# One word of the output through a register of SyncE: eight register instructions at the end of a kernel bound by its loads

## The chip, the cores and the metric

One core of a Trainium2 chip. The time is device microseconds (us) of one execution. A profile's span is shorter than the time of the same execution (711.54 against 709.78 in the kernel before). Times that are read from a trace count from the span's start. Those of single closing instructions are given to 0.01 us, as the trace has them; the views print them to 0.1.

## The reference

```python
def setup_inputs():
    B, N = 8, 2176
    return {"a": np.random.randn(B, N, N).astype(np.float32),
            "b": np.random.randn(B, N, N).astype(np.float32)}

def reference(a, b):
    prod = np.matmul(a, b)
    traces = np.diagonal(prod, axis1=1, axis2=2).sum(axis=-1)
    return traces.astype(np.float32)
```

Only the traces of eight products are wanted, so each is the sum of `a` transposed times `b`, element by element. The output is eight float32 words.

## The kernel before

GpSimd issues the loads, which convert to bf16 on the way. PE transposes blocks of `a`; ScalarE and VectorE copy them out of PSUM; VectorE multiplies with `b` and sums. For the last matrix PE takes a part of the products, and the last row of `b` comes in three pieces. What the change touches is the end:

```python
    # ... const pool: ones, sums [128 x 8], late [128 x 4], result [128 x 8] ...
    late_acc = tiles["late"]
    for n, (x, y) in enumerate(late):
        multiply_reduce(x, y, late_acc[:, n:n + 1])
    multiply_reduce(tiles[f32], trace_ps, late_acc[:, len(late):len(late) + 1])

    total = psum_small.tile([1, BATCH], f32, tag="total")
    nc.tensor.matmul(
        total[:, 0:BATCH - 1], tiles["ones"], tiles["sums"][:, 0:BATCH - 1],
        start=True, stop=True,
    )
    parts = [tiles["sums"][:, BATCH - 1:BATCH]] + [late_acc[:, n:n + 1] for n in range(len(late) + 1)]
    for n, part in enumerate(parts):
        nc.tensor.matmul(
            total[:, BATCH - 1:BATCH], tiles["ones"], part,
            start=(n == 0), stop=(n == len(parts) - 1),
        )
    nc.vector.tensor_copy(out=tiles["result"][:1, :BATCH], in_=total)      # 128 partitions summed by PE
    nc.sync.dma_start(
        out=out.rearrange("(a b) -> a b", a=1),
        in_=tiles["result"][:1, :BATCH],
    )
```

## Time and profile before

| | before |
|---|---|
| time, median of 3 runs | 711.72 us (711.46 to 711.79) |
| span of the profiled run | 709.8 us |
| loads issued by GpSimd, share of 16 engines' span | 100.1% |
| last load lands | 705.60 us |
| VectorE's last copy | 706.91 to 707.06 us |
| SyncE issues the output | 707.10 to 707.42 us |
| end of the span | 709.78 us |

The table is read in two parts. Up to 705.60 the loads set the pace, and other engines have room. From there on a short chain of dependent steps runs to the end. After the kernel's own instructions comes closing code that all carries the line of the launch: SyncE checks off the semaphores of all engines and DMAs, and then all engines meet twice. (A semaphore is a counter that one instruction raises and another waits on.) The lines of the page, the chain, the timeline and SyncE's waits are in the prediction.

### The profile page before, as it was taken

To read this page: it belongs to the slowest core of one execution; us is meant where nothing else is said; L and a number is where in the kernel's file an instruction comes from. 1 tells how busy PE (TensorE), PEld (TensorE's weight loads), DVE (VectorE), ACT (ScalarE), POOL (GpSimd) and SP (SyncE) were. 2 spreads that over 40 slices of the span, in tenths; PEclk is the share of its full clock that TensorE was granted. 3 is DMA by queue.
4 is the path that set the end of the run, shared out by engine and by line. 5 is a ranking of instruction groups with operands and counts; after the bars stand their busy time and mean duration, and the time that the engine had idled before them with its cause. 6 is when DMAs were issued, how large, how long until landed. Compare 5 with 4: busy or idle time off the path is not lost.

```text
span 709.8 us, 3800 instructions
## 1 busy us (share of the span) xinstructions
PE 233.3 (33%) x1406; PEld 221.8 (31%) x1406; DVE 408.9 (58%) x449; ACT 201.6 (28%) x210; POOL 45.2 (6%) x91
## 2 busy tenths in 40 slices
PE   2660025600345003540036400374003630036356
PEld 1660025600344003540036400374003630036355
DVE  0327972279812898219972199621996319963146
ACT  2651015600256002550035500354003630036300
POOL 2000000000000000000000000000000000000010
PEclk9866556755588555885556755666556875567755
DMA  9999999999999999999999999999999999999997
GB/s 220 220 220 219 206 219 219 220 218 206 221 219 218 218 210 218 220 218 214 213 219 219 218 213 214 220 218 216 213 217 219 218 216 212 218 218 216 219 210 139
DMA packets 12116, 152.32 MB, mean 215 GB/s; under 512 B 1346, under 2 KB 1602, under 8 KB 3778
## 3 DMA queue, kind: packets, MB, share of 16 engines
q0 software_dynamic: 11952, 150.97, 100.1%
q1 hardware_dynamic: 146, 1.11, 0.4%
q8 instruction: 11, 0.18, 0.1%
q14 instruction: 7, 0.06, 0.0%
HBM read 303.04 MB, written 0.00 MB: 427 GB/s over the span
## 4 chain that ended last, share of the span: by engine, by line
DMA 52%; issue 43%; POOL 3%; PE 2%; DVE 1%; another core or an unknown queue 0%; POOLq 0%; DVEq 0%
DMA t<-in_a_dram 42%; DMA t<-in_b_dram 6%; DMA b_t<-in_b_dram 3%; POOL t L57 2%; PE ps L136 1%; PE trace_ps L256 1%; DVE scratch L103 0%; DVE at L91 0%; POOL b_t L222 0%; POOLq L57 0%; PE ps L157 0%; POOL identity masks.py:199 0%; PE total L271 0%; POOL identity masks.py:197 0%
## 5 line engine op out<-in xcount | busy, mean ns | idle before, releaser
L103 DVE CUSTOM_DVE_ANT_1 scratch<-at,t 128x2048 bf16<-128x2048 bf16 (+1 forms) x156 | 310.5, 1990 | 85.5 <-DMA t<-in_b_dram 78.9
L136 PE MATMUL ps<-identity,t 128*128 128x128 f32 x1071 | 204.2, 372 | 460.3 <-DMA t<-in_a_dram 297.7
L136 PEld LDWEIGHTS ps<-identity,t 128*128 128x128 f32 x1071 | 193.7, 218 | 468.3 <-issue 302.8
L93 ACT COPY at<-ps 128x1024 bf16<-128x1024 bf16 x208 | 199.2, 1016 | 471.2 <-PE ps L136 471.1
L91 DVE COPY at<-ps 128x1024 bf16<-128x1024 bf16 (+2 forms) x104 | 92.8, 902 | 205.8 <-PE ps L136 198.9
L57 POOL DMA_DIRECT2D t<-in_a_dram x39 | 20.8, 535 | 329.5 <-DVE acc L103 230.2
L57 POOL DMA_DIRECT2D t<-in_b_dram x41 | 21.7, 530 | 304.2 <-PE ps L157 286.5
L256 PEld LDWEIGHTS <-at 128*128 128x128 bf16 x153 | 17.4, 124 | 12.0 <-issue 12.0
L256 PE MATMUL trace_ps<-t,at 128*128 128x128 bf16 x144 | 17.3, 294 | 10.2 <-DMA t<-in_b_dram 10.2
L157 PE MATMUL ps<-identity,t 128*128 128x128 bf16 x170 | 17.0, 224 | 2.2 <-DVE at L91 2.2
L157 PEld LDWEIGHTS <-t 128*128 128x128 bf16 x170 | 13.4, 102 | 3.8 <-issue 3.4
L103 DVE DVE_READ_ACCUMULATOR2_ANT acc<- 128x1 f32 x163 | 13.3, 82 | 0.0
L68 DVE CAST t<-words 128x1088 bf16<-128x1088 f32 x1 | 0.7, 726 | 4.9 <-DMA words<-in_a_dram 4.9
L103 DVE CUSTOM_DVE_ANT_0 scratch<-at,t 128x128 bf16<-128x128 bf16 x7 | 2.0, 291 | 0.2
L67 ACT CAST t<-words 128x1088 bf16<-128x1088 f32 x1 | 1.1, 1098 | 3.7 <-DMA words<-in_a_dram 3.7
L222 POOL DMA_DIRECT2D b_t<-in_b_dram x3 | 1.6, 539 | 3.6 <-PE trace_ps L256 3.6
L256 PE MATMUL trace_ps<-b_t,at 128*128 128x128 bf16 x9 | 1.5, 287 | 0.5 <-DMA b_t<-in_b_dram 0.4
L103 DVE CUSTOM_DVE_ANT_1 scratch<-at,b_t 128x256 bf16<-128x256 bf16 (+1 forms) x3 | 1.5, 510 | 0.2 <-DMA b_t<-in_b_dram 0.2
L248 DVE TENSOR_REDUCE sums<-acc 128x1 f32<-128x22 f32 (+1 forms) x8 | 1.4, 174 | 0.3
L67 ACT ACT_TABLE_LOAD x1 | 1.3, 1283 | 0.7 <-PEq L294 0.7
L271 PE MATMUL total<-late,ones 128*1 128x1 f32 x8 | 0.5, 163 | 0.3 <-DVE late L103 0.3
masks.py:199 POOL TENSOR_SCALAR_AFFINE_SELECT identity<-identity 128x128 f32<-128x128 f32 (+1 forms) x2 | 0.6, 308 | 0.0
(14 smaller groups left out, 2.4 us busy)
## 6 DMA issues: line engine op xcount, KB each, us to landing
t<-in_a_dram POOLq DMA_DIRECT2D x32, 2176.0 KB, 42.3
t<-in_b_dram POOLq DMA_DIRECT2D x31, 2176.0 KB, 47.2
t<-in_b_dram POOLq DMA_DIRECT2D x9, 544.0 KB, 39.5
t<-in_a_dram POOLq DMA_DIRECT2D x7, 544.0 KB, 35.0
words<-in_a_dram SPq DMA_DIRECT2D x1, 1088.0 KB, 5.0
t<-in_b_dram POOLq DMA_DIRECT2D x1, 1088.0 KB, 41.7
b_t<-in_b_dram POOLq DMA_DIRECT2D x1, 256.0 KB, 23.0
b_t<-in_b_dram POOLq DMA_DIRECT2D x1, 160.0 KB, 23.4
```

Of the source, the lines that this page charges most:

```text
L57: issued = nc.gpsimd.dma_start(out=t[:, 0:m, :], in_=rows)
L67: nc.scalar.copy(out=t[:, 0, :half], in_=plain[:, :half])
L68: nc.vector.tensor_copy(out=t[:, 0, half:], in_=plain[:, half:])
L91: nc.vector.tensor_copy(out=dst, in_=src)
L93: nc.scalar.copy(out=dst, in_=src)
L103: nc.vector.tensor_tensor_reduce(out=out, in0=x, in1=y, scale=1.0, scalar=0.0, op0=MUL, op1=ADD, accum_out=acc,)
L136: nc.tensor.transpose(ps[:, n * m + r, :], words[:, r, c0:c0 + step * (P - 1) + 1:step], tiles[f32],)
L157: last_transpose = nc.tensor.transpose(ps16[:, n, r, :], a_t[:, r, c0:c0 + P], tiles[bf16],)
L222: nc.gpsimd.dma_start(out=row[:, lo:hi], in_=b[bi, start:start + P, lo:hi])
L248: nc.vector.reduce_sum(out=tiles["sums"][:, bi:bi + 1], in_=acc[:, :cols], axis=mybir.AxisListType.X)
L256: nc.tensor.matmul(trace_ps, x, y, start=(n == 0), stop=(n == len(pe_work) - 1),)
L271: nc.tensor.matmul(total[:, BATCH - 1:BATCH], tiles["ones"], part, start=(n == 0), stop=(n == len(parts) - 1),)
```

## The change

The intent: seven sums are known some 70 us before the end, so they leave early by DMA. Only the eighth is left for the end, and one word needs no DMA: SyncE loads it into a register and stores it. The word is then read back from the output, so that the program ends after it is known to be in memory.

```diff
-        tiles.update(ones=ones, sums=sums, late=late, result=result)
+        last_sum = const.tile([P, 2], f32, tag="last_sum")
+        tiles.update(ones=ones, sums=sums, late=late, result=result, last_sum=last_sum)
 ...
+    out_words = out.rearrange("(a b) -> a b", a=1)
+    result, last_sum = tiles["result"], tiles["last_sum"]
     total = psum_small.tile([1, BATCH], f32, tag="total")
     nc.tensor.matmul(total[:, 0:BATCH - 1], ...)              # as before
-    parts = ...
+    nc.vector.tensor_copy(out=result[:1, :BATCH - 1], in_=total[:, :BATCH - 1])
+    nc.sync.dma_start(out=out_words[:, :BATCH - 1], in_=result[:1, :BATCH - 1])
+
+    final = psum_small.tile([1, 1], f32, tag="final")
+    parts = ...                                               # the same parts
     for n, part in enumerate(parts):
-        nc.tensor.matmul(total[:, BATCH - 1:BATCH], tiles["ones"], part, ...)
-    nc.vector.tensor_copy(out=tiles["result"][:1, :BATCH], in_=total)
-    nc.sync.dma_start(out=out.rearrange("(a b) -> a b", a=1), in_=tiles["result"][:1, :BATCH])
+        nc.tensor.matmul(final, tiles["ones"], part, ...)
+    nc.vector.tensor_copy(out=last_sum[:1, 0:1], in_=final)
+    words = last_sum.bitcast(mybir.dt.int32)
+    last_word = out_words.bitcast(mybir.dt.int32)[:, BATCH - 1:BATCH]
+    word = nc.sync.alloc_register("word")
+    nc.sync.load(word, words[:1, 0:1])
+    nc.sync.store(last_word, word)
+
+    nc.sync.load(word, last_word)
+    nc.sync.store(words[:1, 1:2], word)
```

More of the change, by code (lines that the diff above doesn't have):

```diff
@@ L268 @@
     )
-    parts = [tiles["sums"][:, BATCH - 1:BATCH]] + [late_acc[:, n:n + 1] for n in range(len(late) + 1)]
+    nc.vector.tensor_copy(out=result[:1, :BATCH - 1], in_=total[:, :BATCH - 1])
+    nc.sync.dma_start(out=out_words[:, :BATCH - 1], in_=result[:1, :BATCH - 1])
+    final = psum_small.tile([1, 1], f32, tag="final")
+    parts = [tiles["sums"][:, BATCH - 1:BATCH]]
+    parts += [late_acc[:, n:n + 1] for n in range(len(late) + 1)]
     for n, part in enumerate(parts):
         nc.tensor.matmul(
-            total[:, BATCH - 1:BATCH], tiles["ones"], part,
-            start=(n == 0), stop=(n == len(parts) - 1),
-        )
-    nc.vector.tensor_copy(out=tiles["result"][:1, :BATCH], in_=total)
-    nc.sync.dma_start(
-        out=out.rearrange("(a b) -> a b", a=1),
-        in_=tiles["result"][:1, :BATCH],
-    )
+            final, tiles["ones"], part, start=(n == 0), stop=(n == len(parts) - 1),
+        )
+    nc.vector.tensor_copy(out=last_sum[:1, 0:1], in_=final)
[6 more added lines that the diff above has]
+    nc.sync.store(words[:1, 1:2], word)
 _INS = ['a', 'b']
```

## The prediction

> **What bounds the kernel now.** I read the page's busy strips first, then the chain that ended last, then the timeline of the last four microseconds, then the waits of SyncE's queue, because the change touches only the end of the program and one spot in its middle.
>
> The page of the kernel before:
>
> ```profile
> span 709.8 us, 3800 instructions
> ...
> DVE  0327972279812898219972199621996319963146
> ...
> DMA  9999999999999999999999999999999999999997
> ...
> q0 software_dynamic: 11952, 150.97, 100.1%
> ...
> HBM read 303.04 MB, written 0.00 MB: 427 GB/s over the span
> ```
>
> The DMA strip is 9 in every slice but the last, and the loads issued by GpSimd fill 100.1% of 16 engines' span, while VectorE is at 58% and PE at 33% (part 1 of the page). For some 705 of 710 us the kernel is the reading of 303 MB. An instruction added to an engine in that stretch is free if it does not delay the release of a buffer. Only the last few microseconds, after the last load lands, are a serial chain in which every added instruction counts in full.
>
> That tail is in the chain that ended last (start, duration, what) between 700 us and the end:
>
> ```profile
> 682.21 23.39 DMA b_t<-in_b_dram
> 705.60 0.04 issue
> 705.64 0.50 PE trace_ps L256 x3
> ...
> 706.34 0.29 DVE scratch L103
> ...
> 706.91 0.15 DVE result L275
> ```
>
> and in the timeline (start, duration, engine, line, operation):
>
> ```profile
> 706.69 0.19 PE L271 MATMUL total<-late,ones 128*1 128x1 f32 x2 [0.28 <-DVE late L103]
> 706.91 0.15 DVE L275 COPY result<-total 1x8 f32<-1x8 f32 x1 [0.28 <-PE total L271]
> 707.10 0.32 SPq L276 DMA_DIRECT2D out_dram<-result  x1
> ```
>
> The last load lands at 705.60, the last sum is copied out of PSUM by 707.06, and SyncE issues the output from 707.10 to 707.42. The span ends at 709.78, so 2.36 us follow the issue. The waits of SyncE's queue (us in total, times, longest) say what is in them:
>
> ```profile
> SPq L276 <- DVE result L275: 705.9, 1, 705.9
> SPq L305 <- PEq L305: 1.4, 2, 0.9
> ...
> SPq L305 <- DMA out_dram<-result: 0.4, 1, 0.4
> ```
>
> The closing code (all of it has the one line L305) waits 0.4 us for the output to land, and 1.4 us in two meetings of all engines. The remaining 2.36 - 0.4 - 1.4 = 0.56 us is SyncE going through its list of closing checks. The first line matters too: SyncE stands idle for 705.9 us, so it has nothing else to do and nothing behind it that could be delayed. The time of that profiled run was 711.54 us, 1.74 over its span; I take this difference as fixed.
>
> **What the Trainium skill says.** "DMA: Bandwidth & Descriptors", section "Latency and other measured facts", gives a floor of about 600 ns for a `tensor_load`, the operation that fills a register of a sequencer from memory. "Runtime: NRT & Kernel Launch", section "Instruction fetch mechanics", says about 200 ns per register for bulk loads, a round trip, and about 73 ns for a store to HBM, which is posted. The same page, section "The ~15µs preamble/postamble breakdown", gives about 1.3 us for a load from HBM of a few words, and calls it one round trip. The trace before has no register load or store, so it neither confirms nor denies these three. For the DMA that is partly relieved, "DMA: Bandwidth & Descriptors", section "Anatomy of one DMA", gives about 2.0 us fixed cost (fitted to DMAs issued by GpSimd). The trace does not agree for this 32-byte write issued by SyncE: it was seen landed after at most 0.56 us of checks and 0.4 us of waiting, so under 1.0 us after its issue ended.
>
> **The change, part by part.**
>
> (1) Seven sums go early. I compared the two built programs' order per engine. The matmul `total<-sums` over the seven columns was already in the middle of PE's stream, and it stays there. What is new is a VectorE copy of 1x7 right after the sums of the seventh matrix, and the DMA of 28 bytes from SyncE. Apart from these and the renamed destination of the last matmuls, the streams of PE, ScalarE, VectorE and GpSimd are instruction for instruction the same. The timeline before shows the spot:
>
> ```profile
> 631.14 1.23 DVE L91 COPY at<-ps 128x1024 bf16<-128x1024 bf16 x1 [1.96 <-PE ps L136]
> ...
> 632.74 0.20 PE L265 MATMUL total<-sums,ones 128*1 128x7 f32 x2
> ...
> 633.65 1.55 DVE L91 COPY at<-ps 128x1024 bf16<-128x1024 bf16 x2 [1.29 <-PE ps L136]
> ```
>
> The matmul ends at 632.94. In the old tail the result copy began at 706.91, 0.03 us after the matmuls before it ended (706.69 + 0.19), and took 0.15; so the new copy runs from about 633.0 to 633.2, inside the 1.29 us in which VectorE is idle anyway (632.37 to 633.65). Cost 0. The 28 bytes go out near 633.4 and are in memory 70 us before the end. Against a 152 MB stream they cost nothing.
>
> (2) Removed from the tail: the issue of the output, 0.32 us, and the wait for its landing, 0.4 us. Both lie on the path: -0.72 us, called -0.7.
>
> (3) The last sum's matmuls and its copy, now into `final` and `last_sum`, have the same number, shapes and waits. The copy of one word rather than eight should again take 0.15 us. Change 0. SyncE starts again near 707.10.
>
> (4) Added to the tail, all in SyncE's stream, in order: load of the word from SBUF; load of the output's address (two registers, a pointer kept in memory); a register addition of 28; the store to the output; the load of the address once more; the addition again; the load of the output word, behind a semaphore that the store raises; the store to SBUF. The diff shows two loads, the built program has four: the address is fetched separately for the store and for the read-back. None can overlap anything, since the first waits for VectorE's last copy and a sequencer goes through its stream in order.
>
> Estimates, from the skill's pages, since no trace here has a duration: the load from SBUF 0.6 (the floor). Each address load between 0.6 and 1.3, taken 1.0. The read-back of a word just written to HBM 1.3 (a full round trip). Two stores at 0.1, two additions at 0.05. Between instructions I add 0.06 each, from the trace: 0.56 us for the eight or so closing steps is 0.07 a step; eight times 0.06 is 0.5. Sum: 0.6 + 2 x 1.0 + 1.3 + 2 x 0.1 + 2 x 0.05 + 0.5 = 4.7 us.
>
> The closing checks and the two meetings of the engines stay as they are: 0.56 + 1.4. The sum of all parts: -0.7 + 4.7 = +4.0 us. With every load at the floor (4 x 0.6 + 0.3 + 0.5 = 3.2) it is +2.5; with 1.3 for all three from HBM (5.3) it is +4.6. I take +3.6, a little under the middle sum, since a pointer load may well be nearer the floor: 711.7 + 3.6 = 715.3 us, or 0.5% more.
>
> **The rivals.**
>
> Register accesses as cheap as other steps of a sequencer. At 0.2 us a load (the skill's figure per register in bulk) the added chain is 4 x 0.2 + 0.3 + 0.5 = 1.6, less 0.7, so 712.6 us. For it: SyncE is otherwise idle, and after the last load lands the memory is quiet. Against it: these are four single loads, not a bulk, each needed before the next step.
>
> Loads much dearer: about 2 us each, the figure for HBM access under load in the first section named above. Then four make 8, with 0.8 beside, less 0.7: +8.1, so 719.8 us. Against it: the strip's last slice is 7 and not 9, the loads being over by 705.60, so nothing should queue before them.
>
> A side effect on the stream of loads. The new tile `last_sum` takes 32 bytes in each partition ahead of the big buffers; in the built program the transposed-matrix buffer moves from byte 17408 to 17440, and every staging buffer moves by 32 with it, off the multiples of 256 that they had. The skill ("DMA: Bandwidth & Descriptors", section "How a descriptor splits into AXI transactions") says a descriptor that does not begin on 256 bytes costs extra beats. If the writing side bound the stream, one transaction more per five or so would be tens of us. Against it: that section's rule is on reading, the read side (HBM) is unchanged, and the writes carry half the bytes (303 MB read against 152 MB moved into SBUF), so they have room. I give it 2%. A little of it, under 1 us, is inside the range.
>
> The read-back hidden behind the engines' meeting. It would be if another engine arrived later than SyncE. But SyncE waits 1.4 us on L305 after the landing while all others have been done since 707.06, so SyncE is the last to come, and its delay passes to the end in full.
>
> **Range and chances.** The range runs from the cheap rival plus a little, 713.0, to loads of about 1.6 us each (6.4 + 0.8 - 0.7 = 6.5), 718.2. 2% is 14.2 us, which would take four loads of over 3.5 us each or the shifted buffers; 2.5% for slower. Faster by 2% has no source, as at most 0.7 us is removed: 0.5%. Within 2%: 97%.
>
> **What would show each step.** Step 1: a 1x7 copy near 633.1 in VectorE's idle time, and the same start of the next copy to 0.1 us against the matmul before it; the strip of DMA all nines again, and the last load landing within 1 us of 705.6. If it lands several us later, the shifted buffers are at work. Step 2: no wait of SyncE for `out_dram` at L317, the new closing line. Step 4: in SyncE's queue, four loads between VectorE's last copy and the closing checks; the distance from the end of that copy to the span's end grows from 2.72 us (707.06 to 709.78) to about 6.3. If it grows by under 1.5 or over 6.5 us, my price of a load is wrong; if it does not grow although the loads are there, SyncE was not the last to arrive.

## More of the kernel before

One view is not there, and it turned out to matter: the closing instructions of the kernel before, here GpSimd's and SyncE's. DRAIN is one of them; what it does is not needed here, only when it ends. The columns are the line, the engine (with q for its sequencer), the operation with its count, the durations in ns as shortest/median/longest, and the first and the last start in us.

```profile
L305 POOLq EVENT_SEMAPHORE  x4: 17/17/17, 709.1 to 709.7; - x4
L305 POOLq DRAIN  x3: 45/95/27027, 682.0 to 709.5; - x3
L305 SPq DRAIN  x3: 7/7/7, 708.2 to 709.3; - x3
```

The first of GpSimd's three DRAINs starts at 682.0, behind GpSimd's last load, and is the long one: 27.027 us, so it ends at 709.03. The first meeting of the engines begins with GpSimd's semaphore instruction at 709.07 (709.1 above); the semaphore it waits on had been raised by SyncE, the last of the other four engines to do so, at 708.30, with the second of SyncE's DRAINs.

## The result, and the profile after

| | before | after |
|---|---|---|
| time, median of 4 runs | 711.69 us (711.46 to 711.79) | 714.20 us (714.12 to 714.25) |
| ratio to before (95% interval) | | 1.0036 (1.0018 to 1.0053) |
| span of the profiled run | 709.8 us | 712.4 us |
| last load lands | 705.60 us | 705.70 us |
| VectorE's last copy ends | 707.06 us | 707.17 us |
| SyncE has done its closing checks | 708.30 us | 711.68 us |
| GpSimd's long DRAIN ends | 709.03 us | 709.14 us |
| the first meeting of the engines begins | 709.07 us | 711.72 us |
| end of the span | 709.78 us | 712.43 us |

Ratios, here and below, are the mean time of one kernel's runs over that of the other's of the same rounds, so not quite the ratio of the medians quoted. The kernel became 2.5 us slower, 0.36%, which counts as the same at a limit of 2%. The prediction was 715.3 in a range of 713.0 to 718.2.

The page after shows the stream of loads as it was:

```profile
span 712.4 us, 3810 instructions
...
DMA  9999999999999999999999999999999999999995
...
q0 software_dynamic: 11952, 150.97, 99.7%
...
HBM read 303.04 MB, written 0.00 MB: 425 GB/s over the span
```

The packets and bytes are the same, and the span is 2.65 us longer: the shares fall a little, and the last slice is emptier. The chain that ended last has its last load landing at 682.33 + 23.38 = 705.71:

```profile
682.33 23.38 DMA b_t<-in_b_dram
705.70 0.04 issue
...
707.03 0.15 DVE L283 COPY last_sum<-final 1x1 f32<-1x1 f32 x1 [0.28 <-PE final L280]
```

(the last of these lines is of the timeline). So everything up to VectorE's last copy is where it was, 0.1 us later. The early half of the change is in the timeline of the kernel after, in the idle time where it was expected:

```profile
632.53 0.20 PE L268 MATMUL total<-sums,ones 128*1 128x7 f32 x2
...
632.76 0.15 DVE L272 COPY result<-total 1x7 f32<-1x7 f32 x1 [0.61 <-PE total L268]
632.94 0.33 SPq L273 DMA_DIRECT2D out_dram<-result  x1
633.61 1.56 DVE L92 COPY at<-ps 128x1024 bf16<-128x1024 bf16 x2 [0.70 <-PE ps L137]
```

The register accesses are not in the timeline, which leaves register instructions out. They are found by the tensors they touch: `last_sum`, then the output's address, then the output (durations in ns, start in us):

```profile
L287 SPq TENSOR_LOAD <-last_sum x1: 476/476/476, 707.2 to 707.2; - x1
L291 SPq TENSOR_STORE last_sum<- x1: 415/415/415, 710.7 to 710.7; - x1
...
L288 SPq TENSOR_LOAD <-out_dram_ptr x1: 1014/1014/1014, 707.7 to 707.7; - x1
L290 SPq TENSOR_LOAD <-out_dram_ptr x1: 850/850/850, 709.3 to 709.3; - x1
...
L288 SPq TENSOR_STORE out_dram<- x1: 348/348/348, 708.9 to 708.9; - x1
L290 SPq TENSOR_LOAD <-out_dram x1: 467/467/467, 710.2 to 710.2; - x1
```

In order: load of the word 0.48, load of the address 1.01, an addition 0.06, store 0.35, load of the address again 0.85, an addition 0.04, load of the word 0.47, store to SBUF 0.42. Their sum is 3.67; with 0.26 between them they run from 707.20 to 711.14, or 3.93 us. Nearly half, 1.86 us, is the address of the output, fetched twice.

SyncE's waits after answer to those of before:

```profile
SPq L287 <- DVE last_sum L283: 73.9, 1, 73.9
...
SPq L317 <- PEq L317: 0.6, 2, 0.5
```

The wait for the output's landing is gone. But the two meetings (L317) now take 0.6 us of SyncE's time and not 1.4 (L305 before), so 0.8 us that the prediction took as fixed went as well. The name PEq in both is the engine that the view puts such a wait down to; GpSimd's line names the true one. After the change:

```profile
L317 POOLq EVENT_SEMAPHORE  x4: 17/17/17, 711.7 to 712.3; - x4
L317 POOLq DRAIN  x3: 45/102/27015, 682.1 to 712.2; - x3
L317 SPq DRAIN  x3: 7/7/13, 711.6 to 711.9; - x3
```

The long DRAIN is as it was and ends at 709.14, but the meeting now begins at 711.72. Before, SyncE was done at 708.30 and the meeting began only when GpSimd's DRAIN was over, at 709.07: SyncE had 709.03 - 708.30 = 0.73 us to spare. After, SyncE is done at 711.68, and GpSimd waits for it.

The account: from VectorE's last copy to SyncE's last check it was 1.24 us (707.06 to 708.30) and is 4.51 (707.17 to 711.68), so 3.27 more; of these, 0.73 were hidden behind GpSimd's DRAIN. 3.27 - 0.73 = 2.54 us, against 2.51 between the medians. (The two profiled spans differ by 2.65; 0.11 of that is the last load's later landing, which moved GpSimd's DRAIN as well.)

### The profile page after: what moved, and what is told of

Same layout as the page of the kernel before. It is cut to its first block, busy times and chain, and to the rows that moved or that the text cites. A ratio compares the mean times of both kernels' runs of the same rounds, so it can differ in the third digit from the quotient of the medians.

```text
span 712.4 us, 3810 instructions
## 1 busy us (share of the span) xinstructions
PE 231.1 (32%) x1406; PEld 219.3 (31%) x1406; DVE 408.9 (57%) x450; ACT 201.6 (28%) x210; POOL 45.0 (6%) x91
## 4 chain that ended last, share of the span: by engine, by line
DMA 51%; issue 42%; POOL 3%; PE 2%; DVE 1%; another core or an unknown queue 0%; POOLq 0%; DVEq 0%
DMA t<-in_a_dram 42%; DMA t<-in_b_dram 6%; DMA b_t<-in_b_dram 3%; POOL t L57 2%; PE ps L137 1%; PE trace_ps L257 1%; DVE scratch L104 0%; DVE at L92 0%; POOL b_t L223 0%; POOLq L57 0%; PE ps L158 0%; POOL identity masks.py:199 0%; PE final L280 0%; POOL identity masks.py:197 0%
## 5 line engine op out<-in xcount | busy, mean ns | idle before, releaser
L137 PE MATMUL ps<-identity,t 128*128 128x128 f32 x1071 | 202.1, 369 | 462.4 <-DMA t<-in_a_dram 338.5
L137 PEld LDWEIGHTS ps<-identity,t 128*128 128x128 f32 x1071 | 191.3, 218 | 470.6 <-issue 344.0
```

Of the source, the lines that this page charges most:

```text
L137: nc.tensor.transpose(ps[:, n * m + r, :], words[:, r, c0:c0 + step * (P - 1) + 1:step], tiles[f32],)
```

## The experiments

The theory, called P: the end is set by whoever is last to the first meeting, and in the kernel before that is GpSimd with its closing DRAIN, near 709.1 us. The rival, D: a DMA that SyncE issues late makes the meeting itself last some 0.7 us longer, and GpSimd plays no part; taking that DMA away is what shortened the meeting. Both fit the two traces. The 95% intervals of ratios below are about 0.0015 wide to each side, or 1 us, so for smaller differences the single runs and the traces have to speak.

**The eighth word never stored.** The changed kernel, without its register part; the eighth word is wrong.

```diff
-    words = last_sum.bitcast(mybir.dt.int32)
-    ...                       # all loads and stores of registers
```

> The changed kernel without the whole register part: seven sums go out early by DMA, the eighth is computed but never stored (its word of the output is wrong on purpose). SyncE then has nothing to do at the end and comes to the first closing meeting of the engines near 707.5 us. Theory P (in the kernel before the end was set by GpSimd, whose closing drain runs until about 709.1 us whatever SyncE does): time as before, 711.7 us, although a DMA of the output and 0.4 us of waiting are gone. Rival D (a DMA that SyncE issues late makes the meeting itself last about 0.7 us longer, and GpSimd plays no part): the meeting is over by about 708.1, so the time falls to about 710.0 us.

Measured: 711.56 us (711.53 to 711.62), ratio 1.0000 (0.9986 to 1.0013). SyncE was done with its checks at 707.32, and yet:

```profile
SPq L309 <- PEq L309: 2.4, 2, 2.0
...
L309 POOLq EVENT_SEMAPHORE  x4: 17/17/17, 709.1 to 709.7; - x4
L309 POOLq DRAIN  x3: 45/95/27024, 682.1 to 709.6; - x3
```

(the first line is of SyncE's waits, the others of GpSimd's closing code). SyncE waits 2.0 us in the first meeting, with no late DMA of its own, until GpSimd's DRAIN is over. P holds. D expected 710.0, outside the interval (710.0 would be 0.9977). It also says what the last word could have gained at most: nothing. With no output at the end at all, the time is that of the kernel before.

**The store without the read-back.**

```diff
     nc.sync.store(last_word, word)
-
-    nc.sync.load(word, last_word)
-    nc.sync.store(words[:1, 1:2], word)
```

> The changed kernel with the store but without the read-back (second address load, addition, load of the output word, store to SBUF). From the trace these four run from 709.27 to 711.13 us, so both P and D expect 1.9 us less than the changed kernel: 712.3 us, still 0.6 over the kernel before. If a load only looks long because SyncE waits for the store to be done, less than 1.9 us would be saved.

Measured: 711.90 us (711.78 to 712.24), correct, ratio 1.0005 (0.9992 to 1.0019). That saves 2.3 of the changed kernel's time where 1.9 was expected, and the interval does not tell it from the kernel before. The trace shows where most of the further 0.4 comes from:

```profile
L288 SPq TENSOR_STORE out_dram<- x1: 84/84/84, 708.7 to 708.7; - x1
```

The store took 0.084 us and not 0.348. In the changed kernel it raises a semaphore for the read-back to wait on; here nothing waits for it, and it raises none. So 0.26 us of the read-back's price is in the line before it. (The output was correct in these five runs, though nothing in this kernel waits for the word to land.) SyncE was done at 709.36 and the meeting began at 709.40, against GpSimd's DRAIN ending at 709.05: SyncE is the last by 0.3 us, and by the medians the kernel is slower than before by about as much.

**The early half alone.** Seven sums early, the eighth by a DMA of one word; the buffers stay shifted by 32 bytes.

```diff
-    words = last_sum.bitcast(mybir.dt.int32)
-    ...                       # all loads and stores of registers
+    nc.sync.dma_start(out=out_words[:, BATCH - 1:BATCH], in_=last_sum[:1, 0:1])
```

> Seven sums early by DMA, the eighth late by a DMA of one word: the part of the change without registers, with the new tile and so with the buffers shifted by 32 bytes. P and D: 711.7 us, as before. If the early copy, the early DMA or the shifted buffers cost anything (the rival of the prediction), it shows here alone: more than 711.9 us and a last load landing later than 705.8 us.

Measured: 711.58 us (711.53 to 711.65), correct, ratio 1.0000 (0.9986 to 1.0014); the last load landed at 705.58. The early copy, the early DMA and the shift of the buffers cost nothing that can be seen. The whole 2.5 us is the register part.

**The read-back twice.**

```diff
     nc.sync.load(word, last_word)
     nc.sync.store(words[:1, 1:2], word)
+    nc.sync.load(word, last_word)
+    nc.sync.store(words[:1, 1:2], word)
```

> The changed kernel with the read-back done twice. If every register access is on the path that sets the end, the second read-back costs the 1.9 us that the first one takes in the trace: 716.1 us. If a part of the first read-back is waiting for the store to reach memory, the second is cheaper, and its load of the output word is shorter than 0.47 us.

Measured: 716.10 us (715.98 to 716.20), correct, ratio 1.0063 (1.0050 to 1.0077): 1.9 more than the changed kernel, as expected. The loads of the output word:

```profile
L290 SPq TENSOR_LOAD <-out_dram x1: 458/458/458, 710.1 to 710.1; - x1
L292 SPq TENSOR_LOAD <-out_dram x1: 455/455/455, 712.1 to 712.1; - x1
```

The second is as long as the first. So the first read-back does not wait inside its load for the store to arrive. Whether the longer store, the one that raises a semaphore, waits for that is not shown.

**A load and a store beside the output's DMA.** From here on the kernel before is changed. The scheduler placed both accesses behind the DMA's issue.

```diff
     nc.vector.tensor_copy(out=tiles["result"][:1, :BATCH], in_=total)
+    word = nc.sync.alloc_register("word")
+    nc.sync.load(word, tiles["result"].bitcast(mybir.dt.int32)[:1, 0:1])
     nc.sync.dma_start(...)
+    nc.sync.store(tiles["spare"].bitcast(mybir.dt.int32)[:1, 0:1], word)
```

> The kernel before, with one register load from SBUF and one register store to SBUF (about 1.0 us together) in SyncE's stream after the output's DMA is issued. Of it 0.4 us falls into the wait for the DMA's landing, so SyncE comes to the meeting about 0.6 us later, near 708.9 us. P (GpSimd's drain ends near 709.1): no change, 711.7 us. D (the meeting takes 0.77 us after SyncE's arrival): 712.3 us.

Measured: 711.59 us (711.55 to 711.65), correct, ratio 1.0001 (0.9987 to 1.0014). SyncE was done at 708.91, 0.61 later than in the kernel before, and the meeting began when it always does:

```profile
L310 POOLq EVENT_SEMAPHORE  x4: 17/17/17, 709.2 to 709.8; - x4
L310 POOLq DRAIN  x3: 45/102/27012, 682.1 to 709.6; - x3
```

P expected no change. D's 712.3 is inside the interval of the ratio, but all five runs lie 0.6 below it, and the trace shows the meeting at 709.16, not 0.77 after SyncE's 708.91.

**Three loads and stores ahead of the output's DMA.**

```diff
     nc.vector.tensor_copy(out=tiles["result"][:1, :BATCH], in_=total)
+    word = nc.sync.alloc_register("word")
+    # three times, to three words of spare:
+    nc.sync.load(word, tiles["result"].bitcast(mybir.dt.int32)[:1, 0:1])
+    nc.sync.store(tiles["spare"].bitcast(mybir.dt.int32)[:1, 0:1], word)
```

> The kernel before, with three pairs of register load and store (about 0.97 us each, 2.9 us in all) in SyncE's stream ahead of the output's DMA. SyncE comes to the meeting near 711.2 us. P: the first 0.75 us of this is hidden behind GpSimd's drain, so +2.15, 713.85 us. D: +2.9, 714.6 us.

Measured: 712.86 us (712.80 to 713.00), correct, ratio 1.0019 (1.0005 to 1.0033): +1.34, where 2.15 was expected. The size of a pair was wrong, not the theory. The output's DMA was issued at 709.09 and not at 707.10, so the three pairs took 2.0 us and not 2.9:

```profile
L279 SPq TENSOR_LOAD <-result x1: 468/468/468, 707.1 to 707.1; - x1
L281 SPq TENSOR_LOAD <-result x1: 278/278/278, 707.9 to 707.9; - x1
L283 SPq TENSOR_LOAD <-result x1: 263/263/263, 708.5 to 708.5; - x1
```

Only the first load costs 0.47, and the stores between them 0.23 to 0.25. With the measured 2.0, P gives 2.0 - 0.73 = 1.27 and D 2.0; 1.34 was found. The late DMA is present here, and the meeting still began at 710.33, 0.03 after SyncE's last check at 710.30: the 0.77 of D is not there.

**The output issued by GpSimd.** This moves GpSimd's DRAIN itself.

```diff
-    nc.sync.dma_start(
+    nc.gpsimd.dma_start(
         out=out.rearrange("(a b) -> a b", a=1),
```

> The kernel before, with the output's DMA issued by GpSimd in place of SyncE. If GpSimd's closing drain ends a fixed time after the landing of the last DMA that it issued (705.6 to 709.07, 3.5 us), the output landing near 709 moves the drain's end to about 712.5 and the time to about 715.1 us. If the drain has some fixed length of its own or ends with the loads, the time stays within 1 us of 711.7.

Measured: 717.37 us (717.25 to 717.45), correct, ratio 1.0082 (1.0068 to 1.0096). SyncE was done at 709.41, and all waited for GpSimd:

```profile
L305 POOLq EVENT_SEMAPHORE  x4: 17/17/17, 714.9 to 715.5; - x4
L305 POOLq DRAIN  x3: 46/95/7482, 707.4 to 715.3; - x3
...
out_dram<-result POOLq DMA_DIRECT2D x1, 0.0 KB, 1.6
```

(the last line is the DMA's issue, with 1.6 us to landing). The DRAIN took 7.48 us from 707.36 and ended at 714.84, and the time followed it: +5.8. That GpSimd's DRAIN sets the end is so shown a third way. How long it lasts was expected wrongly: it ended 5.9 us after the landing at 708.97, and not 3.4 after, as it does behind the loads (709.03 - 705.60). In the ten other kernels here, in which GpSimd's last DMA is a load, the DRAIN ended 3.43 us after that load's landing each time, to 0.01 us, while the landing lay anywhere from 705.58 to 705.79 and the DRAIN's length from 27.01 to 27.16. So behind the loads the DRAIN's end follows the last landing and is not set by a length of its own. What it waits for after the landing, and why it was 5.9 us behind the output, stays open.

**Prices of register accesses.** The changed kernel with a row of loads behind it, each followed by a store of its registers to SBUF, so that none is removed as unused.

```diff
+    nc.sync.load([low, high], words[:1, 0:2])        # then stores of low, high
+    nc.sync.load(low, words[:1, 0:1])                # ... and so for each
+    nc.sync.load(low, ints[:, 0:1])                  # first word of the output
+    nc.sync.load([low, high], ints[:, 0:2])
+    nc.sync.load(low, a.bitcast(mybir.dt.int32)[0, 0:1, 0:1])
```

> The changed kernel with a row of further register accesses after the read-back, each load with a store of its registers to SBUF: two registers in one load from SBUF; one from SBUF; one from the output's first word (an address load before it); two from the output's first words; one from the input a. The time only grows by their sum, estimated at 10 us: 724. What counts is the single durations. If a load costs by the register, both loads of two registers take about 0.95 us and all of one about 0.47, whether from SBUF or HBM, and the address loads of 0.85 to 1.0 us are just two registers. If it is the address table that is slow, loads of two registers from SBUF and output stay near 0.47.

Measured: 722.68 us (722.50 to 722.71), correct, ratio 1.0156 (1.0140 to 1.0172), so +8.5 over the changed kernel, and not 10.

```profile
L297 SPq TENSOR_LOAD <-last_sum x1: 480/480/480, 711.2 to 711.2; - x1
L300 SPq TENSOR_LOAD <-last_sum x1: 272/272/272, 712.3 to 712.3; - x1
...
L302 SPq TENSOR_LOAD <-out_dram x1: 471/471/471, 713.9 to 713.9; - x1
L304 SPq TENSOR_LOAD <-out_dram x1: 839/839/839, 716.0 to 716.0; - x1
...
L307 SPq TENSOR_LOAD <-in_a_dram x1: 628/628/628, 718.6 to 718.6; - x1
```

From the output, two registers cost 0.84 and one 0.47, so there the second register added 0.37. But one register from the input `a` took 0.63 and not 0.47, so a register from HBM has no single price. The address loads of all runs took 0.83 to 0.85 us right behind the store to the output and 0.99 to 1.12 behind an access to SBUF; that they cost so much because they are two registers fits, but is not shown. From SBUF two at once took 0.48 and not 0.95: the first of the two theories can hold for HBM alone. And one register from SBUF is 0.27 in one place and 0.47 in another.

**A test of the price list.**

```diff
+    # old is the tile late; each load is followed by stores of its registers to spare
+    nc.sync.load(r0, old[:1, 0:1])                   # twice; the scheduler puts these two ahead of the load of last_sum
+    nc.sync.load([r0, r1], old[:1, 0:2])
+    nc.sync.load([r0, r1, r2, r3], old[:1, 0:4])
+    nc.sync.load(r0, last_word)
+    nc.sync.load(r1, last_word)
```

> Made to test a price list read from the runs so far. SBUF: load 0.27 us for one register, 0.2 for each further one; store 0.23. HBM: load 0.45 for one register and 0.4 for the second; store 0.35 where a semaphore follows it, 0.08 where none does. And 0.2 more for any access whose predecessor went to another memory, or that comes after a long pause. So: first load of late (L297) 0.47, second (L299) 0.27; the load of last_sum (L289) 0.27 here, because two SBUF accesses stand before it, where it took 0.48 in the changed kernel; two registers at once from SBUF (L301) 0.48; four at once (L304) 0.88; all SBUF stores after SBUF 0.23; address loads after an SBUF store (L309, L310) 1.0, the word loads after them 0.46, the SBUF stores after those 0.40. Rival: what is slow is the wait for a semaphore ahead of an access; then L289, which still waits for VectorE, stays at 0.48, and the load of two registers at 0.27. Time about 722 us on either.

Measured: 720.55 us (720.46 to 720.68), correct, ratio 1.0126 (1.0109 to 1.0142). It came out 1.5 lower than expected; the first loads ran before VectorE's last copy, and the load of four was cheap.

```profile
L297 SPq TENSOR_LOAD <-late x1: 474/474/474, 705.3 to 705.3; - x1
L299 SPq TENSOR_LOAD <-late x1: 291/291/291, 706.1 to 706.1; - x1
L301 SPq TENSOR_LOAD <-late x1: 482/482/482, 711.0 to 711.0; - x1
L304 SPq TENSOR_LOAD <-late x1: 299/299/299, 712.1 to 712.1; - x1
L289 SPq TENSOR_LOAD <-last_sum x1: 273/273/273, 707.3 to 707.3; - x1
```

The load of `last_sum` (L289) still waits for VectorE, and takes 0.27 with SBUF accesses ahead of it, where it took 0.48 after a long pause. So it is not the wait that is dear, and the rival falls; that the first access to a memory is dear, by about 0.2 us, fits. The stores fit (0.23 after SBUF, 0.40 after a load from HBM), and so do the last address loads (1.0). The price by the register does not hold for SBUF: four at once (L304) took 0.30, where 0.88 was expected. Why two at once took 0.48 in both runs, behind an SBUF store that itself came after HBM, is not settled: each was also the first load from SBUF since loads from HBM, and no run separates this from the two registers.

**No version beats the kernel before.** A kernel that stores nothing at the end takes as long as it, so the way in which the last word goes out can't gain anything here; only an earlier end of GpSimd's DRAIN could, which behind the loads means an earlier last landing, and no run here tried that. The address could perhaps be fetched before VectorE's last copy; no run tried this, and by the same argument it could win at most the 0.3 us that the kernel without the read-back loses.

## Why the prediction was right

- **What bounds the kernel**: right. The last load landed at 705.70 against 705.60, and the early half alone ran in 711.58.
- **Step 1, the early sums cost nothing**: right, with the copy at 632.76 inside VectorE's idle time. The "tens of us" that it put on its rival, the shifted buffers, were not worked out, and the early half alone shows none of them.
- **Step 2, removed: 0.7 us**: right as far as SyncE's own stream goes (0.32 of issue and 0.4 of waiting are gone), but they were worth nothing to the time. GpSimd's DRAIN covered them, as the kernel with nothing stored at the end shows.
- **Step 3, the last matmuls and the copy unchanged**: right, 0.15 us again.
- **Step 4, four loads and two stores in a row, 4.7 us**: the list of instructions was right, the sum 0.8 too large. The read-back was put at 1.3 and took 0.47; the two stores at 0.1 each and took 0.35 and 0.42; the address loads at 1.0 and took 1.01 and 0.85; the load from SBUF at 0.6 and took 0.48; the gaps at 0.5 and took 0.26. That the sum is no further off is in part luck: the read-back was 0.83 too dear, and the stores together 0.56 too cheap.
- **The step that failed**: "SyncE is the last to come, and its delay passes to the end in full", with which the prediction dismissed a rival, and with it the 1.4 us of the two meetings as a part that stays. In the kernel before, GpSimd came last, 0.73 us after SyncE; the first 0.73 us of SyncE's delay passed unseen. The view that was read, SyncE's waits, names PE for this, and PE had been done since 706.88. Looking at each engine's closing instructions would have shown the DRAIN of 27 us. For the same reason it was wrong that after the last landing every added instruction counts in full.

The two errors, 0.8 in the accesses and 0.73 in the slack, both made the prediction too high: the full sum was +4.0 and 4.0 - 0.8 - 0.73 is 2.5. It was shaded to +3.6 by a guess, and the range held the result. That its sum with every load at the floor was +2.5 too is a coincidence: it leaves out the 0.73. Nor did its own signs catch the slack: the time from VectorE's last copy to the end of the span grew from 2.72 to 5.26 us, which is by 2.54, and only growth under 1.5 or over 6.5 was to call a load's price wrong.

## What to carry to other kernels

At the end of a program ask of every engine when its own closing code is done, sequencer instructions included, before pricing the path of the one that was looked at: here an engine whose last work was issued 27 us earlier was the last to come. A word through a register was no cheaper than a small DMA when it went to the output: SyncE was ready for the meeting 2.28 us after VectorE's last copy with the store alone, and 1.24 with the DMA in the kernel before. The address was fetched for each access (0.83 to 1.12 us), and a read-back doubles that; a store that nothing waits for cost 0.08 us in the one run that had it, one that raises a semaphore 0.32 to 0.35.

## What the Trainium skill lacked or had wrong

- "VectorE: DVE Perf Modes", section "The DRAIN you can't avoid", speaks of the DRAINs of the closing code as about 12 ns, constant, on all five engines. SyncE's here took 7 to 15 ns, but GpSimd's first took 27.0 to 27.2 us behind its last loads, ending 3.43 us after the landing in each of the ten runs that end with a load, and 7.48 us behind a DMA of the output, ending 5.9 us after its landing. No page says that this DRAIN can set a program's end.
- "DMA: Bandwidth & Descriptors", section "Latency and other measured facts", gives a floor of about 600 ns for a `tensor_load`. Loads of one register took 0.26 to 0.48 us from SBUF and 0.46 to 0.47 from the output in HBM; only the one from the input `a` took 0.63.
- "Runtime: NRT & Kernel Launch", section "Instruction fetch mechanics": the store of about 73 ns fits the one that raises no semaphore (84 ns); it lacks that the same store with a semaphore took 0.32 to 0.35 us, and that a store to SBUF with one took 0.23 to 0.26, or about 0.40 after a load from HBM. About 200 ns per register does not fit HBM here (0.47 for one and 0.84 for two from the output, 0.63 for one from `a`) nor SBUF (0.30 for four).
- No page says that the store or load of a word of the output carries a load of its address with it, 0.83 to 1.12 us each time, nor that a load of one register from SBUF took some 0.2 us more when it was the first (0.47 against 0.27).
